# Feed-forward slabs whose weight sums are formed in place by accumulating transfers: 60 slabs a part in a staggered order, and the last tiles at half depth

## The chip, the cores and the metric

The kernel runs on one core of one Trainium2 chip. The metric is the device time of one execution in microseconds, lower is better. A core has TensorE (PE, matrix multiplication; PEld is its weight load), VectorE (DVE), ScalarE (ACT), GpSimd (POOL) and SyncE (SP). They run side by side, each taking its own instructions in a fixed order, and wait for each other through semaphores. Transfers are started by an engine's queue (here SP's, and POOL's where a transfer adds to what lies at its destination) and carried by sixteen DMA engines.

## What is computed

A trunk of two decoder layers on 256 tokens of width 2048. Layer 0 mixes tokens by causal pooling and attends to a memory; layer 1 uses differential attention over shared keys and values, and the memory again. Each layer ends in a squared-ReLU feed-forward part, which is what the change touches:

```
def squared_relu_mlp(h, w1, w2):
    z = jax.nn.relu(h @ w1)
    return (z * z) @ w2
...
x = x + squared_relu_mlp(rms_norm(x, ffn_norm[i]), w_ff1[i], w_ff2[i])
```

`w1` is 2048 x 8192 and `w2` 8192 x 2048, so `z` has 64 groups of 128 channels, and the result 16 groups.

## The kernel before

**Split numbers.** Each fp32 operand is used as a high part (rounded by a cast) and a low part (the rest). A product is high x high + high x low + low x high. Weights arrive in blocks of 128 x 128. Eight blocks make one 512 KB row of `wst`, the weights in order of use, which SP loads. ScalarE casts the high part into `hi_ring` (L178), VectorE subtracts to get the low part into `lo_ring` (L181). Each ring has six slots of 512 columns. A plain quad of four blocks takes one slot.

**Feed.** `Plan` records on a dry pass which quads and slab jobs are used in which order. `Feed.fill(job)` prepares a job and up to three entries ahead of it, as far as slots are free (`_prepare` L190, `fill` L225), and `Feed.load` (L122) issues the loads three or four rows ahead of that. The order of instructions on each engine is fixed when the program is built; the order in which the code writes them is its main input, and TensorE's instructions of neighbouring jobs can be interleaved.

**Plain tiles.** `up_tile` makes one group of 128 channels of `z` from 16 blocks of `w1` (`a_part`: for each block a 512-column matmul with the high weights, L433, and a 256-column one with the low weights, L435). What comes out of PSUM is copied (L761), summed, passed through ReLU and squared into one of the `stage` buffers, then split into `z` (`convert`). Two neighbouring groups of `z` also give four sums of quarters, split into `sit` (`combine`, L792-L803). `c_tile` (L447-L449) does a block in three 256-column matmuls that add up in one place, so nothing has to be summed after it.

**Slabs.** Most of `z @ w2` is computed by a two-by-two scheme with seven products in place of eight. A slab is a pair `i` of groups of `z` (256 channels) against 1024 columns of the result, the right half (group 0) or the left half (group 1). It holds four weight quarters of 128 x 512: left and right column quads for two channel groups. Its seven products, three matmuls of 512 columns each, add into seven PSUM banks, and are issued as four jobs: job 0 (two products, with the left column of quarters), job 1 (one product, with the sum T1), job 2 (two products, with the second sum T2 and one quarter), job 3 (two products). Before job 1 stands K, which makes T2 on VectorE (L204). The weight sums in the kernel before: T1 is made by a plain load and an accumulating transfer (`first_sum`, L153), T2 by K, the two operands of job 3 by one subtraction over 1024 columns after job 0's split (L218).

**Order.** The `up_tile` calls 0 to 63 make `z`; between their quarters `due` issues slab jobs by a table of due times in tiles (`early`, a constant rate, `late`). The jobs are slab after slab, 0 1 2 3. The same pairs serve both halves: four slabs of one group, then four of the other, and where the group changes, `swap` (L932, L924) copies the seven banks out to `keep` buffers and the other group's back. After the last slab of the left half `close_left` forms the left result, and `turn_left` transposes it into the residual. Pairs 0 to 23 are in both halves, 24 to 31 only in the right one: 56 slabs a part. The rest of the left half (eight tiles of 128 columns, channel groups 48 to 63) is done by `down_tile` at the end, in `last`, with the last sixteen slab jobs in between; `finish_banks` then forms the right half, and its transposes (L1016) and additions (L1017) follow eight and ten steps later. A step (`tick`) is one quad of blocks, or in `last` also one job.

Of the kernel before, what the change touches and what calls it, by code (L numbers as in the profile page):

```python
# [17 lines left out]
P = 128  # L18
T = 256
# [36 lines left out]
class Plan:  # L56
# [13 lines left out]
    def close(self):  # L70
        prep = []
        for job in self.jobs:

            if job[0] == "S" and job[2] == 0:
                prep.append(("K", job[1]))
            prep.append(job)
# [4 lines left out]
        for p in prep:  # L81
            if p[0] == "K":
                self.loads += [("S", p[1], 0), ("S", p[1], 1)]
            elif p[0] == "N" and p[1] % 2 == 0:
                self.loads.append(("N", p[1] // 2))
# [13 lines left out]
class Feed:  # L99


    def __init__(self, tc, wst, wpool, rows, plan, dry):
# [7 lines left out]
        self.t1 = None  # L110
        self.loads_ahead = LOADS
        self.t1_of = [None] * 3
# [9 lines left out]
    def load(self, upto):  # L122
        while self.lp < min(upto, len(self.plan.loads)):
# [6 lines left out]
            elif r[2] and r[1] % 2:  # L130
                t = self.spare
# [4 lines left out]
            elif r[2] == 0:  # L136
                if r[1] % PER_PART == 0:
                    self.first_sum(r[1])
                self.nc.sync.dma_start(t, self.wst[h])
                if (r[1] + 1) % PER_PART:  # L140
                    self.first_sum(r[1] + 1)
# [5 lines left out]
    def first_sum(self, n):  # L147
        i = n % len(self.t1)
        assert self.t1_of[i] is None
        self.t1_of[i] = n  # L150
        left, right = (self.wst[self.plan.row["S", n, c], :, 0:512] for c in range(2))
        self.nc.sync.dma_start(self.t1[i], left)
        self.nc.gpsimd.dma_start(self.t1[i], right, accum_op=ALU.add)  # L153
# [36 lines left out]
    def _prepare(self, p):  # L190
        sub, add = self.nc.vector.tensor_sub, self.nc.vector.tensor_add
# [9 lines left out]
        ra, rb = self.raw[("S", p[1], 0)], self.raw.get(("S", p[1], 1))  # L201
        t1 = self.t1[p[1] % len(self.t1)]
        if p[0] == "K":
            one = sub(rb[:, 0:512], t1, rb[:, 512:1024])  # L204
            if p[1] % PER_PART:
                self.order(one, self.last_low.ins.name)
# [5 lines left out]
        src, n = ((ra, 2), (t1, 1), (rb, 2), (ra, 2))[p[2]]  # L212
        if not self._split(p, src, n):
            return False
        if p[2] == 0:
            t2 = rb[:, 0:512].unsqueeze(1).to_broadcast([P, 2, 512])
            two = ra.rearrange("p (a c) -> p a c", a=2)
            sub(two, t2, two)  # L218
        if p[2] == 1:
            self.t1_of[p[1] % len(self.t1)] = None  # L220
        if p[2] == 3:
            del self.raw[("S", p[1], 0)], self.raw[("S", p[1], 1)]
# [69 lines left out]
def program(ctx, tc, plan, dry, xT, memT, par, lam, cst, wst, yT):  # L292
# [437 lines left out]
    def ffn(l, xs, tags, done):  # L730
# [12 lines left out]
        stage = [staged[:, T * j : T * j + T] for j in range(8)]  # L743
        sums = [room[:, 512 * j : 512 * j + 512] for j in range(2)]
        feed.t1 = [room[:, 1024 + 512 * j : 1536 + 512 * j] for j in range(3)]
        outs = [room[:, 2560 + 512 * j : 3072 + 512 * j] for j in range(2)]
        feed.spare = room[:, 3584:4608]
        keep = [room[:, 4608 + 512 * j : 5120 + 512 * j] for j in range(7)]
# [5 lines left out]
        z_done, sit_done = set(), set()  # L754
# [11 lines left out]
        def convert(j):  # L766
            a = stage[j % 8]
# [19 lines left out]
            def combine():  # L787
                sit_free[i % 4] = False
                a11, a21 = stage[2 * i % 8][:, 0:P], stage[2 * i % 8][:, P:T]
                a12, a22 = stage[(2 * i + 1) % 8][:, 0:P], stage[(2 * i + 1) % 8][:, P:T]  # L790
                s1, s2, s3, s4 = (sums[i % 2][:, c * P : c * P + P] for c in range(4))
                nc.vector.tensor_add(s1, a21, a22)  # L792
                nc.vector.tensor_sub(s3, a11, a21)
                nc.vector.tensor_sub(s2, s1, a11)
                nc.vector.tensor_sub(s4, a12, s2)
# [14 lines left out]
        def up_tile(i, ps, between=None):  # L810
# [18 lines left out]
            def square():  # L829
                nc.scalar.activation(stage[i % 8], y[:, 0:T], AF.Square)  # L830
# [4 lines left out]
        def down_tile(n, ps, between=None):  # L835
            ks = range(3 * NK, 4 * NK)
            if l == 1 and n == 7:
# [32 lines left out]
        def slab_jobs(g, i, again, end):  # L870
# [14 lines left out]
            def summed(c):  # L885
# [8 lines left out]
                ((5, lambda: summed(2)), (6, lambda: plain(1, 1))),  # L894
# [16 lines left out]
        def open_banks():  # L911
            tags = (("mm", 3), ("mm", 3), ("mm", 3), ("s", 2), ("s", 2), ("o", 1), ("t", 1))
            for p, (tag, bufs) in enumerate(tags):
# [739 lines left out]
```

## Time and profile before

| | us |
|---|---|
| median of three runs | 2005.55 (2004.99 to 2006.17) |
| the profiled execution | 2005.08 |
| its span, first to last instruction | 2003.3 |
| TensorE, VectorE, ScalarE, GpSimd busy | 1997.0, 1757.3, 1500.4, 149.9 |
| accumulating transfers | 112, each 256 KB |

A row of a timeline gives start, length, engine, line, operation, output<-input, shapes and count; in brackets the idle time before it and what ended it. A group row gives the count, then busy time and the mean of one in ns, then idle time before. A row of a stretch gives busy time and instruction count of each engine. Matmuls overlap, so the distance from one start to the next is their cost, not the length that a row prints. Lines such as L181 are lines of the kernel printed above.

### The profile page before, as it was taken

The page shows a single profiled execution, that of the slowest core. Times are in us where ns is not written, and L with a number is a line of the kernel's source. Part 1 is how long each engine was busy: PE and PEld are TensorE (multiplying, and loading weights), DVE is VectorE, ACT ScalarE, POOL GpSimd, SP SyncE. Part 2 cuts the span into 40 slices and gives each one's busy share as a digit, 9 for nine tenths or more (in the row PEclk, how much of TensorE's full clock was granted, in tenths as well). Part 3 has the DMA queues.
Part 4 walks back from the last instruction along what each step waited for, and adds up shares of the span by engine and source line. Part 5 has one row for each costly group of instructions (what it writes and reads, how often), then busy time and mean ns, then how long its engine had stood idle before and what let it go on. Part 6 is the DMA issues. An engine that isn't in the chain of part 4 may idle for free.

```text
span 2003.3 us, 31841 instructions
## 1 busy us (share of the span) xinstructions
PE 1997.0 (100%) x10534; PEld 1702.3 (85%) x10534; DVE 1757.3 (88%) x3089; ACT 1500.4 (75%) x2791; POOL 149.9 (7%) x179
## 2 busy tenths in 40 slices
PE   9999999999999999999999999999999999999999
PEld 8888888888888888888888888888888888888888
DVE  8888888989989899999765698878989899999987
ACT  7765577787887878778665699567787878888775
POOL 0001310000000000000000000320000000000000
PEclk9999999999999999999999999999999999999999
DMA  8555576777777776755566534567777777777764
GB/s 315 177 185 193 189 220 214 233 218 233 227 227 227 226 231 209 228 181 186 184 233 196 169 127 135 197 198 225 222 227 227 222 235 225 228 229 215 223 222 132
DMA packets 142725, 420.09 MB, mean 210 GB/s; under 512 B 16096, under 2 KB 18784, under 8 KB 142560
## 3 DMA queue, kind: packets, MB, share of 16 engines
q1 hardware_dynamic: 126288, 388.69, 57.9%
q0 software_dynamic: 16128, 29.37, 8.9%
q8 instruction: 82, 1.34, 0.3%
q14 instruction: 83, 0.68, 0.1%
q10 hardware_dynamic: 144, 0.01, 0.0%
HBM read 415.90 MB, written 2.10 MB: 209 GB/s over the span
## 4 chain that ended last, share of the span: by engine, by line
PE 97%; DVE 1%; ACT 1%; issue 0%; DMA 0%; DVEq 0%; ACTq 0%
PE x_bank L433 24%; PE x_bank L435 12%; PE p L865 9%; PE p L868 9%; PE p L867 9%; PE wo L433 6%; PE wo L435 3%; PE u L433 2%; PE ff L433 1%; PE u L435 1%; PE q L467 1%; PE q L469 1%; PE k L467 1%; PE q L468 1%; PE k L469 1%; PE v L467 1%
## 5 line engine op out<-in xcount | busy, mean ns | idle before, releaser
L178 ACT CAST hi_ring<-raw 128x512 fp32r<-128x512 f32 x1001 | 610.5, 621 | 270.4 <-PE x_bank L433 66.1
L181 DVE TENSOR_TENSOR lo_ring<-raw,hi_ring 128x512 fp32r<-128x512 f32 x1001 | 680.7, 695 | 109.0 <-ACT hi_ring L178 96.9
L433 PE MATMUL x_bank<-fx,hi_ring 128*128 128x512 f32 x1952 | 610.7, 394 | 0.0
L435 PEld LDWEIGHTS x_bank<-fx,lo_ring 128*128 128x128 f32 x1952 | 366.0, 188 | 86.2 <-DVE lo_ring L181 3.1
L181 DVE TENSOR_TENSOR lo_ring<-slab,hi_ring 128x1024 fp32r<-128x1024 f32 x280 | 342.2, 1222 | 58.0 <-ACT hi_ring L178 56.2
L178 ACT CAST hi_ring<-slab 128x1024 fp32r<-128x1024 f32 x280 | 294.3, 1052 | 121.6 <-PE x_bank L433 65.3
L435 PE MATMUL x_bank<-fx,lo_ring 128*128 128x256 f32 x1952 | 384.4, 278 | 0.2 <-DVE lo_ring L181 0.2
L433 PEld LDWEIGHTS x_bank<-fx,hi_ring 128*128 128x128 f32 x1952 | 318.1, 189 | 23.7 <-ACT room L761 1.6
L153 POOL DMA_DIRECT2D room<-in_w x112 | 96.8, 868 | 1127.5 <-DMA room<-in_w 1111.7
L865 PE MATMUL p<-hi_ring,sit 128*128 128x512 f32 x448 | 177.0, 395 | 0.7 <-ACT hi_ring L178 0.5
L867 PE MATMUL p<-hi_ring,sit 128*128 128x512 f32 x448 | 175.3, 391 | 0.0
L868 PE MATMUL p<-lo_ring,sit 128*128 128x512 f32 x448 | 174.5, 390 | 0.1
L433 PE MATMUL wo<-cat,hi_ring 128*128 128x512 f32 x512 | 161.8, 397 | 0.3 <-DVE rc L404 0.3
L181 DVE TENSOR_TENSOR lo_ring<-room,hi_ring 128x512 fp32r<-128x512 f32 x168 | 144.9, 864 | 6.9 <-ACT hi_ring L178 6.9
L178 ACT CAST hi_ring<-room 128x512 fp32r<-128x512 f32 x168 | 128.6, 766 | 23.7 <-PE x_bank L433 17.1
L865 PE MATMUL p<-hi_ring,z 128*128 128x512 f32 x336 | 131.3, 391 | 0.0
L867 PE MATMUL p<-hi_ring,z 128*128 128x512 f32 x336 | 131.1, 390 | 0.0
L868 PE MATMUL p<-lo_ring,z 128*128 128x512 f32 x336 | 130.7, 389 | 0.0
L435 PEld LDWEIGHTS wo<-cat,lo_ring 128*128 128x128 f32 x512 | 95.9, 188 | 22.0
L435 PE MATMUL wo<-cat,lo_ring 128*128 128x256 f32 x512 | 101.5, 279 | 0.0
L868 PEld LDWEIGHTS p<-lo_ring,sit 128*128 128x128 f32 x448 | 84.1, 188 | 20.3 <-DVE lo_ring L181 2.3
L865 PEld LDWEIGHTS p<-hi_ring,sit 128*128 128x128 f32 x448 | 84.0, 187 | 11.9 <-ACT hi_ring L178 3.3
(374 smaller groups left out, 3350.8 us busy)
## 6 DMA issues: line engine op xcount, KB each, us to landing
raw<-in_w SPq DMA_DIRECT2D x500, 512.0 KB, 4.3
slab<-in_w SPq DMA_DIRECT2D x112, 512.0 KB, 4.3
room<-in_w SPq DMA_DIRECT2D x168, 256.0 KB, 3.3
room<-in_w POOLq DMA_DIRECT2D x112, 256.0 KB, 5.8
slab<-in_w SPq DMA_DIRECT2D x56, 256.0 KB, 4.5
memraw<-in_mem SPq DMA_DIRECT2D x5, 512.0 KB, 4.5
resid<-in_x SPq DMA_DIRECT2D x8, 256.0 KB, 5.7
out_y<-resid SPq DMA_DIRECT2D x16, 128.0 KB, 1.9
```

What stands on the lines that cost most here:

```text
L153: self.nc.gpsimd.dma_start(self.t1[i], right, accum_op=ALU.add)
L178: self.last_cast = self.nc.scalar.copy(hi, src)
L181: low = self.nc.vector.tensor_sub(lo, src, hi.bitcast(F32))
L433: nc.tensor.matmul(ps, hi, xs[:, k, :], start=first and c == 0, stop=False)
L435: nc.tensor.matmul(ps[:, T : 2 * T], lo, xs[:, k, 0:T], start=False, stop=last and c == len(ks) - 1,)
L467: nc.tensor.matmul(ps[t], x[t][1], hi, start=k == 0, stop=False)
L468: nc.tensor.matmul(ps[t], x[t][0], hi, start=False, stop=False)
L469: nc.tensor.matmul(ps[t], x[t][0], lo, start=False, stop=k == NK - 1)
L865: nc.tensor.matmul(ps, a[1], hi, start=new, stop=False, **again)
L867: nc.tensor.matmul(ps, a[0], hi, start=False, stop=False, **again)
L868: nc.tensor.matmul(ps, a[0], lo, start=False, stop=end, **again)
```

## The change

Each slab keeps its sums in its own two buffers. Job 0's operand (left quarters, one above the other) is loaded plainly; after its split an accumulating transfer adds the right upper quarter to its first half, which then is T1. K adds T1 to the right lower quarter to form T2, in a buffer `second` (three of them) into which only the right lower quarter was loaded. After job 2's split a second accumulating transfer adds the right upper quarter to that half, and VectorE adds the left lower quarter to T2, so that job 3 finds its operands in place. Some signs of the sums of `z` and of the results change with it. The stage buffers are six instead of eight.

The jobs are staggered: a period holds job 0 of slab p+1, jobs 1 and 2 of slab p, and job 3 of slab p-1. Pairs 0 to 27 are in both halves, 28 to 31 only in the right: 60 slabs a part, with two more changes of the group. Periods are 0.97 tiles after the early ones. `down_tile` covers channel groups 56 to 63 only, tiles 3 to 7 in the three-matmul form; twelve jobs are left for `last`, in groups of 5, 3, 2 and 2 before tiles 0 to 3, and `finish_banks` stands before tile 3. Tile 4 of the up-projection uses another bank, and the slab banks are opened in two parts.

```diff
@@ class Plan, class Feed
-            if job[0] == "S" and job[2] == 0:
+            if job[0] == "S" and job[2] == 1:
                 prep.append(("K", job[1]))
...
-                if r[1] % PER_PART == 0:
-                    self.first_sum(r[1])
                 self.nc.sync.dma_start(t, self.wst[h])
-                if (r[1] + 1) % PER_PART:
-                    self.first_sum(r[1] + 1)
...
-    def first_sum(self, n):
-        i = n % len(self.t1)
-        assert self.t1_of[i] is None
-        self.t1_of[i] = n
-        left, right = (self.wst[self.plan.row["S", n, c], :, 0:512] for c in range(2))
-        self.nc.sync.dma_start(self.t1[i], left)
-        self.nc.gpsimd.dma_start(self.t1[i], right, accum_op=ALU.add)
+    def add_right(self, n, t):
+
+        h = self.plan.row["S", n, 1]
+        self.nc.gpsimd.dma_start(t, self.wst[h, :, 0:512], accum_op=ALU.add)
...
-            one = sub(rb[:, 0:512], t1, rb[:, 512:1024])
+            one = add(rb[:, 0:512], ra[:, 0:512], rb[:, 512:1024])
...
-        src, n = ((ra, 2), (t1, 1), (rb, 2), (ra, 2))[p[2]]
+        src, n = ((ra, 2), (ra, 1), (rb, 2), (rb, 2))[p[2]]
...
         if p[2] == 0:
-            t2 = rb[:, 0:512].unsqueeze(1).to_broadcast([P, 2, 512])
-            two = ra.rearrange("p (a c) -> p a c", a=2)
-            sub(two, t2, two)
+            self.add_right(p[1], ra[:, 0:512])
+        elif p[2] == 2:
+            self.add_right(p[1], rb[:, 512:1024])
+            add(rb[:, 0:512], rb[:, 0:512], ra[:, 512:1024])
...
@@ ffn
         def down_tile(n, ps, between=None):
-            ks = range(3 * NK, 4 * NK)
-            if l == 1 and n == 7:
+            ks = range(56, 64)
+            assert all(k in z_done for k in ks)
+            if n >= 3:
                 c_tile(ps, "w_ff2", l, n, ks, z)
...
-        for h in range(6):
-            for g in (0, 1) if h % 2 == 0 else (1, 0):
-                slabs += [(g, 4 * h + i, g == h % 2) for i in range(4)]
-        slabs += [(0, i, False) for i in range(24, 32)]
-        jobs = [(s, j) for s in range(len(slabs)) for j in range(4)]
+        for h, first in enumerate((0, 1, 0, 1, 0, 1, 1)):
+            for g in (first, 1 - first):
+                slabs += [(g, 4 * h + i, g == first) for i in range(4)]
+        slabs += [(0, i, False) for i in range(28, 32)]
+        early = (4.5, 6, 8, 10, 11.2, 12.2, 13.2, 14.2, 15.2, 16.2, 17.4, 18.4)
...
+            return 18.4 + 0.97 * (p - 10)
+
+        jobs = []
+        for p in range(-1, len(slabs) + 1):
+            for j, s in enumerate((p + 1, p, p, p - 1)):
+                if 0 <= s < len(slabs):
+                    when_due = tiles_at(p) + j * (tiles_at(p + 1) - tiles_at(p)) / 4
+                    jobs.append((when_due, s, j))
...
-        early = (4, 6, 8, 10, 11.5, 12.5, 13.5, 14.5, 15, 16, 17.5, 19, 20.5)
-        late = (58, 59.5, 61, 62.5, 64)
...
-        ends = (
-            (1, 1, 1, 0), (1, 1, 1, 0), (1, 1, 1, 1), (1, 0, 1, 0), (1, 0, 1, 0), (2, 0, 0, 0),
-        )
...
             for n in range(8):
-                if n < 6:
-                    some(ends[n][0])
-                if n == 5:
+                for c in range((5, 3, 2, 2, 0, 0, 0, 0)[n]):
+                    one_job()
+                    tick()
+                    if c == 2 and turns:
+                        turn_left(turns.pop(0))
+                assert n == 0 or not turns
+                if n == 3:
                     finish_banks()
-                ps = bank() if n < 6 else mmt("ff2")
-                down_tile(n, ps, between(n) if n < 6 else None)
+                down_tile(n, bank() if n < 4 else mmt("ff2"))
```

109 lines of the change are left out of this document (56 added, 53 removed).

## The prediction, made before the changed kernel was run

> **What bounds the kernel now.** First the profile page: its head, the row of engines, and the chain of work that ended last.
>
> ```profile
> span 2003.3 us, 31841 instructions
> ...
> PE 1997.0 (100%) x10534; PEld 1702.3 (85%) x10534; DVE 1757.3 (88%) x3089; ACT 1500.4 (75%) x2791; POOL 149.9 (7%) x179
> ...
> PE 97%; DVE 1%; ACT 1%; issue 0%; DMA 0%; DVEq 0%; ACTq 0%
> ```
>
> TensorE is idle for 6.3 us in all, and 97% of the chain is its own work. So the time moves by matmul time first, and then by gaps that the change opens. Second, the busy time of the engines by stretch (PE, PEld, DVE, ACT, POOL; then granted clock, DMA share, GB/s): the start of the first feed-forward part, the close of its left half, the end of that part, the middle of the second part.
>
> ```profile
> 260.00:300.00 40.00, 39.82 (x220) 34.14 (x219) 33.87 (x66) 29.37 (x58) 1.90 (x3) 1.00 0.73 206
> 750.00:800.00 50.00, 49.66 (x254) 41.09 (x253) 47.77 (x71) 43.24 (x73) 4.19 (x5) 1.00 0.70 215
> 910.00:920.00 10.00, 10.00 (x61) 8.76 (x60) 10.00 (x20) 7.68 (x15) 0.00 (x0) 1.00 0.63 201
> 1420.00:1820.00 400.00, 400.00 (x2056) 339.76 (x2055) 372.02 (x564) 321.76 (x542) 32.77 (x38) 1.00 0.76 228
> ```
>
> TensorE loses 0.18 us at the start and 0.34 us at the close, and nothing in 400 us of the middle, where VectorE is busy 93%, ScalarE 80% and the DMA engines 76%. At the end of the first part VectorE is at 100%. These are the engines that a change can run into.
>
> The profiled execution took 2005.08 us, 1.8 us more than its span; the median of the three runs is 0.47 us above it. I work out a difference and add it to the median, 2005.55.
>
> **Matmul time.** Rows of TensorE from the end of the second part: the first and, after twelve slab matmuls, the next row; the first of sixteen plain blocks and the row after them; the first block of a tile of three short matmuls per block, and its sixth following one.
>
> ```profile
> 1978.09 0.40 PE L865 MATMUL p<-hi_ring,sit 128*128 128x512 f32 x1
> ...
> 1980.82 0.61 PE L433 MATMUL x_bank<-z,hi_ring 128*128 128x512 f32 x2
> ...
> 1986.38 0.62 PE L433 MATMUL ff<-z,hi_ring 128*128 128x512 f32 x2
> ...
> 1991.96 0.27 PE L1016 MATMUL ct<-const,c_b 128*128 128x128 f32 x1
> ...
> 1993.19 0.28 PE L447 MATMUL ff<-z,hi_ring 128*128 128x256 f32 x1
> ...
> 1995.34 0.28 PE L447 MATMUL ff<-z,hi_ring 128*128 128x256 f32 x1
> ```
>
> Twelve slab matmuls take 2.73 us, so a slab's 21 take 4.78 us. Sixteen plain blocks take 5.58 us. A slab stands for 16 blocks: 0.80 us saved. There are four more slabs in each of two parts: **-6.4 us**. Five of the last eight tiles of each part now use the three-matmul form: 2.15/6 = 0.358 us a block against 0.349, on 80 blocks less the 8 that had it: **+0.7**.
>
> **VectorE and the steady stretch.** Each slab loses one subtraction over 1024 columns (L218) and gains one addition over 512; the K operation keeps its 512. Back to back they take (chain of waits, start and length):
>
> ```profile
> 762.26 0.60 DVE slab L204
> ...
> 763.46 1.14 DVE lo_ring L181
> ```
>
> That is 0.54 us less VectorE work a slab. Slabs now come every 0.97 tiles: 0.97 x 5.58 + 4.78 = 10.2 us, before every 1.04 tiles, 10.6. VectorE's 93% of 10.6 is 9.85; less 0.54 and some 0.3 for the shorter tile it is 9.0 of 10.2, 88%. TensorE had no gap here, so this gains nothing. SyncE issues two loads a slab instead of three; GpSimd issues two accumulating transfers instead of one. Those, from the view of their line and the page's queues:
>
> ```profile
> L153 POOL DMA_DIRECT2D room<-in_w x112: 853/862/1203, 256.9 to 1939.3; - x112
> L153 POOLq EVENT_SEMAPHORE  x106: 17/17/43, 256.2 to 1938.7; - x106
> ...
> DMA to landing us min/median/max: 3.6/5.8/8.5
> ```
>
> ```profile
> q1 hardware_dynamic: 126288, 388.69, 57.9%
> q0 software_dynamic: 16128, 29.37, 8.9%
> ```
>
> The queue releases the last one at 1938.7 and the issue starts at 1939.3: 0.6 us, then 5.8 us to landing. By the shares, an accumulated MB takes 8.9% x 2003 / 29.37 = 6.1 us of all engines, a plain one 3.0. In a 10.2 us period 0.52 MB and 1.80 MB make 8.6 us: 84% instead of 76%. From one low split through the accumulation to the next: 0.1 + 0.6 + 5.8 + a cast of 1.05 + a split of 1.22 = **8.8 us**. The staggered order leaves five jobs, 1.25 periods = 12.7 us, between job 0 and job 1 and between job 2 and job 3. So the second transfer is hidden here, by 3.9 us and the lead of the preparation; beyond that VectorE stands in its queue with the splits of the plain blocks behind it.
>
> Two more exchanges of the seven banks per part cost ScalarE fourteen copies each:
>
> ```profile
> L924 ACT COPY p<-room 128x512 f32<-128x512 f32 x56 | 33.0, 610 | 0.0
> L932 ACT COPY room<-p 128x512 f32<-128x512 f32 x56 | 31.7, 595 | 0.3
> ```
>
> 8.4 us each, where two periods leave some 4 us idle. In the 400 us above such exchanges cost nothing, at the close 0.34 us: four new ones cost 0 to 1.4, I take **+0.4**, nearer the many. At the start VectorE waited for the first sums:
>
> ```profile
> DVE slab L204 <- DMA room<-in_w: 10.6, 2, 5.4
> ```
>
> Now K of slab 0 comes two tiles after job 0, so the 0.2 us of TensorE go: **-0.2**. The same wait in the timeline:
>
> ```profile
> 259.39 0.40 ACT L386 ACTIVATE rs_t<-rs_h 128x256 f32<-128x256 f32 x1
> ...
> 263.92 0.69 DVE L204 TENSOR_TENSOR slab<-room,slab 128x512 f32<-128x512 f32 x1 [5.14 <-DMA room<-in_w]
> ...
> 264.53 0.42 DVE L329 SCALAR_TENSOR_TENSOR rs_t<-st_x,rs_t 128x256 f32<-128x256 f32 x1
> ```
>
> The operation at 264.53 was ready at 259.8 and stood behind it: the order on an engine is fixed beforehand, and did not foresee the landing.
>
> **The closing stretch** (59.2 is job 2 of slab 59, T0 to T7 the last tiles). The order is 58.0 57.1 57.2 56.3 59.0, T0, 58.1 58.2 57.3, T1, 59.1 59.2, T2, 58.3 59.3, sums, T3 to T7. Between the low matmuls of 59.2 and 59.3 lie only six matmuls (1.37), T2 (2.79) and six more (1.37): 5.5 us against a chain of 8.8. What covers the rest is how early 59.2's split is done. Three low splits of a job 2, each with the first matmul that reads it (first, one of the middle, last of 112):
>
> ```profile
> 279.25 1.22 DVE L181 TENSOR_TENSOR lo_ring<-slab,hi_ring 128x1024 fp32r<-128x1024 f32 x1
> 283.27 0.39 PE L868 MATMUL p<-lo_ring,sit 128*128 128x512 f32 x1
> ...
> 712.73 1.21 DVE L181 TENSOR_TENSOR lo_ring<-room,hi_ring 128x1024 fp32r<-128x1024 f32 x1
> 715.23 0.39 PE L868 MATMUL p<-lo_ring,sit 128*128 128x512 f32 x1
> ...
> 1975.68 1.22 DVE L181 TENSOR_TENSOR lo_ring<-room,hi_ring 128x1024 fp32r<-128x1024 f32 x1 [0.51 <-ACT hi_ring L178]
> 1978.55 0.39 PE L868 MATMUL p<-lo_ring,sit 128*128 128x512 f32 x1
> ```
>
> The leads are 2.8, 1.3 and 1.65 us, mean 1.9. 8.8 - 5.5 - 1.9 = 1.4 us a part: **+2.8**. Behind 59.3 in TensorE's queue stand T3's matmuls, on the other two engines T3's splits. Bounds: a landing at 3.6 gives 0, no lead 3.3 a part, a landing at 8.5 with the mean lead 4.1.
>
> VectorE from 58.0 to the split of 59.3: eight splits of 1.14, eight of 0.60, eight more 512-column operations, eight of 256 columns and four of 128:
>
> ```profile
> 266.08 0.34 DVE z L776
> ```
>
> ```profile
> L792 DVE TENSOR_TENSOR room<-stage 128x128 f32<-128x128 f32 x64 | 18.3, 286 | 5.4 <-ACT stage L830 5.4
> ```
>
> 9.1 + 4.8 + 4.8 + 2.7 + 1.1 = 22.5 us. TensorE has 13.0 (jobs) + 0.5 + 8.4 (T0 to T2) + 0.9 (two transposes of the left half) = 22.8. That is 99%; before, sixteen jobs lay among six full tiles. Between 0 (the lead covers it) and the lost lead, 1.9 a part, I take 0.4: **+0.8**.
>
> The last eight transposes now come after T7, since T3 to T7 make only ten steps:
>
> ```profile
> 1992.12 0.87 PE ct L1016 x8
> ```
>
> ```profile
> 1999.32 0.28 PE L449 MATMUL ff<-z,lo_ring 128*128 128x256 f32 x1
> ...
> 1999.64 0.42 DVE L840 TENSOR_TENSOR room<-ff,r_x 128x256 f32<-128x256 f32 x1 [2.01 <-PE ff L449]
> 2000.10 0.42 DVE L841 TENSOR_TENSOR resid<-resid,room 128x256 f32<-128x256 f32 x1
> ```
>
> Now 1.2 us lead from the last matmul to the last addition. After: 0.6 for four transposes and their wait, two additions of 0.60, then T7's two, 0.9: 2.7. Less the 0.87 of transposes that left the path: **+0.7**, in the second part alone.
>
> **Sum:** -6.4 + 0.7 - 0.2 + 0.4 + 2.8 + 0.8 + 0.7 = -1.2, so **2004.3 us**.
>
> The Trainium skill, page "DMA: Bandwidth & Descriptors", section "Anatomy of one DMA — SWDGE (gpsimd) path", gives such a transfer about 2.0 us plus its bytes at 436 GB/s, 2.6 us for 256 KB as an estimate. The row above says 5.8 at the median and never under 3.6, so the trace does not agree. By that figure the wait before 59.3 would vanish and the sum be 2.8 us lower.
>
> **Rivals.**
>
> *In time.* A landing of 4.4 us or less at 59.3, or T3's matmuls placed before it, removes the 2.8, and with it VectorE's 0.8. For it: the minimum of 3.6, and a DMA share of only 43 to 63% at the end of a part. Against it: the median of 5.8, and the order that did not foresee the landing at the start. 2004.3 - 3.6 = 2000.7 us.
>
> *VectorE has no lead at the close* (slower). It decides when VectorE's work in the closing stretch exceeds TensorE's: at 99%, a few waits for ScalarE do it. Then each 59.3 costs 1.9 more (+3.8), and in the first part, where twelve tiles' splits for the next layer at 0.40 add 4.8 us and VectorE is at 100% already, half of these are not hidden (+2.4). 2010.5 us. Against it: TensorE lost nothing at 910 to 920, at that same 100%.
>
> *The transfers queue* (slower). At 84% the landing would have to grow from 5.8 to over 11 us for the steady stretch to wait; the longest of 112 is 8.5. If a third of the 120 slabs waited 0.4 us, +16: 2020 us.
>
> **Numbers.** My forecast 0.43, in time 0.30, no lead 0.21, queueing 0.06. This kernel's measurement can tell about 0.2%, 4.0 us, from no change. My forecast's own range is 2001 to 2008, nearly all of it no change; faster is the first rival and 0.03 of the forecast, 0.33; slower the two others, 0.27. The range 1999.6 to 2010.8 leaves out the queue, the upper half of the no-lead case and the lowest part of the first rival.
>
> **What would show it.** Products: 60 slabs at 4.78 us. A ScalarE or VectorE wait for an accumulating transfer about 20 us before the end of a part, with a TensorE gap of 1 to 2 us, shows the term of 59.3; no such gap, and 2000 to 2001, shows the first rival; VectorE at 100% there with gaps at several jobs, the second; long landings and waits in mid-part, the third. If the middle's gaps are not near 0, the step that the stagger hides the transfers is wrong.

## The result, and the profile after

The changed kernel takes 2009.41 us (median of 13 runs, 2007.76 to 2012.57) against 2005.40 us for the kernel before (13 runs beside it, 2004.32 to 2006.50): a ratio of 1.0020, 95% interval 1.0013 to 1.0028. The forecast was 2004.3. The profiled execution took 2008.45 us, with a span 3.2 us longer than before's. One of the executions behind this document, at a granted clock of 0.654, took 2822.13 us; it belongs to experiment 6, whose ratio leaves it out.

First the page of the changed kernel: its head, the row of engines, the two queues, and the chain.

```profile
span 2006.5 us, 32110 instructions
...
PE 1991.4 (99%) x10510; PEld 1697.4 (85%) x10510; DVE 1728.1 (86%) x3096; ACT 1526.8 (76%) x2838; POOL 260.9 (13%) x307
...
q1 hardware_dynamic: 110160, 357.22, 54.2%
q0 software_dynamic: 34560, 62.93, 19.0%
...
PE 68%; issue 22%; POOL 4%; ACT 2%; DMA 2%; DVE 1%; POOLq 0%; SPq 0%; DVEq 0%; ACTq 0%
```

TensorE's busy time fell by 5.6 us and the span still grew: TensorE is now idle for 15.1 us and not 6.3. TensorE's own work was 97% of the chain and is 68%, but that is no measure of the loss: another 22% of the chain is "issue", in which an engine on it waited for nothing that the profile shows, while TensorE is idle for less than 1% of the span. VectorE has less to do in all (1728.1 against 1757.3 us). So the question is where the idle time lies, and it lies in few places. From the starts of the first matmuls of each stage in both traces:

| stage, us | before | after | difference |
|---|---|---|---|
| start, to the first feed-forward matmul | 251.56 | 251.19 | -0.4 |
| first feed-forward part, to the first `k` matmul | 675.62 | 675.05 | -0.6 |
| `k` tiles, to the first `v` matmul | 67.60 | 70.45 | +2.85 |
| the rest, to the second part | 328.75 | 328.77 | 0.0 |
| second part, to the last matmul | 675.78 | 675.72 | -0.1 |
| from there to the end of the span | 4.0 | 5.3 | +1.35 |

The first part has 20 matmuls of 512 columns fewer and 16 of 256 columns more. The second, where one tile had three matmuls a block before, has 4 and 16 fewer. At 0.227 and 0.116 us from start to start that is -2.7 and -2.8 us, -5.4 in all, where the prediction had -5.7. So some 2 to 2.6 us a part are given back inside the parts, and 4.2 us behind them. The busy time by stretch (PE, PEld, DVE, ACT, POOL; granted clock, DMA share, GB/s) of the changed kernel shows the places:

```profile
440.00:460.00 20.00, 18.73 (x95) 15.32 (x94) 17.39 (x29) 13.81 (x24) 3.46 (x4) 1.00 0.84 227
...
910.00:920.00 10.00, 8.68 (x71) 8.26 (x71) 10.00 (x21) 7.80 (x16) 0.00 (x0) 1.00 0.37 116
924.00:934.00 10.00, 8.68 (x49) 7.27 (x48) 9.87 (x23) 7.96 (x18) 0.00 (x0) 1.00 0.29 106
...
1515.00:1535.00 20.00, 18.88 (x95) 15.43 (x94) 17.17 (x29) 13.84 (x24) 3.46 (x4) 1.00 0.87 233
1975.00:1985.00 10.00, 8.36 (x42) 6.37 (x41) 7.69 (x13) 6.18 (x11) 0.86 (x1) 1.00 0.54 144
```

Five stretches, and two kinds. At 910 and 924, around the end of the first part, VectorE is full (10.00 and 9.87 of 10). At 440, 1515 and 1975 TensorE waits though VectorE is not full: something is late there. The two in mid-part were not expected at all.

The stall at 450, in TensorE's timeline, then ScalarE's (start, length, engine, line, operation, and in brackets the idle time before it and who ended it):

```profile
450.10 0.39 PE L867 MATMUL p<-lo_ring,sit 128*128 128x512 f32 x1
450.97 0.50 PE L864 MATMUL p<-hi_ring,z 128*128 128x512 f32 x1 [0.48 <-ACT hi_ring L176]
451.30 0.40 PE L866 MATMUL p<-hi_ring,z 128*128 128x512 f32 x1
452.48 0.50 PE L867 MATMUL p<-lo_ring,z 128*128 128x512 f32 x1 [0.79 <-DVE lo_ring L179]
```

```profile
445.47 1.05 ACT L176 CAST hi_ring<-room 128x1024 fp32r<-128x1024 f32 x1 [1.45 <-PE p L866]
449.35 0.62 ACT L176 CAST hi_ring<-raw 128x512 fp32r<-128x512 f32 x1 [2.83 <-DMA raw<-in_w]
449.87 1.04 ACT L176 CAST hi_ring<-room 128x1024 fp32r<-128x1024 f32 x1
```

The matmuls wait for the cast from `room` at 449.87 (a job 3), and that cast was ready; it stood on ScalarE behind the cast of a plain row, which waited 2.83 us for its transfer. Start to start, TensorE lost 1.60 us here and 1.45 us at 1524.

The wait before 59.3 in the second part, which the prediction had, on ScalarE:

```profile
1978.30 0.62 ACT L176 CAST hi_ring<-raw 128x512 fp32r<-128x512 f32 x1 [1.08 <-issue]
1981.47 1.04 ACT L176 CAST hi_ring<-room 128x1024 fp32r<-128x1024 f32 x1 [2.54 <-DMA room<-in_w]
```

TensorE was idle for 1.35 us before 1982.56 and 0.29 before 1983.82; from start to start it lost 2.0 us. In the first part there is no such gap. Over the whole kernel three casts waited for one of the 240 accumulating transfers, all three in a closing stretch (896.60, 905.69 and this one); from the view of the transfers' line:

```profile
  ACT hi_ring L176: 3.7, 3
...
DMA to landing us min/median/max: 3.6/5.5/8.1
```

The end of the first part. TensorE, then VectorE just ahead of the second gap:

```profile
917.06 0.33 PE L1015 MATMUL ct<-const,c_b 128*128 128x128 f32 x1 [0.68 <-DVE c_a L1004]
918.03 0.33 PE L1015 MATMUL ct<-const,c_a 128*128 128x128 f32 x1 [0.64 <-ACT c_a L967]
...
932.81 0.73 PE L466 MATMUL k<-lo_ring,x_kv 128*128 128x512 f32 x2 [1.32 <-DVE lo_ring L179]
```

```profile
928.74 1.28 DVE L1016 TENSOR_TENSOR resid<-resid,ct 128x512 f32<-128x512 f32 x2
930.14 1.68 DVE L326 SCALAR_TENSOR_TENSOR x_kv<-resid,param,x_kv 128x256 fp32r<-128x256 f32 x4
931.75 0.42 DVE L839 TENSOR_TENSOR room<-ff,r_x 128x256 f32<-128x256 f32 x1
932.08 0.68 DVE L179 TENSOR_TENSOR lo_ring<-raw,hi_ring 128x512 fp32r<-128x512 f32 x1
```

First the transposes wait for the final sums and their scaling (1.70 us from start to start, in two gaps). Then, once they are done, their additions and the low halves of `x_kv` come in one lump, 3.4 us of VectorE, and the low split that the next `k` matmul needs is the last of the four lines.

### The profile page after: what moved, and what is told of

The parts are those of the page before. It is cut to its first block, busy times and chain, and to the rows that moved or that the text cites. A ratio compares the mean times of both kernels' runs of the same rounds, so it can differ in the third digit from the quotient of the medians.

```text
span 2006.5 us, 32110 instructions
## 1 busy us (share of the span) xinstructions
PE 1991.4 (99%) x10510; PEld 1697.4 (85%) x10510; DVE 1728.1 (86%) x3096; ACT 1526.8 (76%) x2838; POOL 260.9 (13%) x307
## 4 chain that ended last, share of the span: by engine, by line
PE 68%; issue 22%; POOL 4%; ACT 2%; DMA 2%; DVE 1%; POOLq 0%; SPq 0%; DVEq 0%; ACTq 0%
PE x_bank L430 13%; PE x_bank L432 7%; PE wo L430 6%; PE p L864 5%; PE p L867 5%; PE p L866 5%; PE wo L432 3%; PE u L430 2%; POOL room L151 2%; POOL slab L151 2%; PE ff L430 1%; PE u L432 1%; PE q L464 1%; PE q L466 1%; PE q L465 1%
## 5 line engine op out<-in xcount | busy, mean ns | idle before, releaser
L176 ACT CAST hi_ring<-raw 128x512 fp32r<-128x512 f32 x969 | 595.2, 620 | 258.7 <-PE wo L430 58.7
L179 DVE TENSOR_TENSOR lo_ring<-raw,hi_ring 128x512 fp32r<-128x512 f32 x969 | 663.9, 694 | 111.2 <-ACT hi_ring L176 99.3
L179 DVE TENSOR_TENSOR lo_ring<-room,hi_ring 128x1024 fp32r<-128x1024 f32 x240 | 293.2, 1222 | 50.8 <-ACT hi_ring L176 47.2
L176 ACT CAST hi_ring<-room 128x1024 fp32r<-128x1024 f32 x240 | 252.8, 1053 | 91.1 <-PE p L866 50.0
L179 DVE TENSOR_TENSOR lo_ring<-slab,hi_ring 128x512 fp32r<-128x512 f32 (+1 forms) x240 | 228.9, 954 | 50.8 <-ACT hi_ring L176 48.3
L176 ACT CAST hi_ring<-slab 128x512 fp32r<-128x512 f32 (+1 forms) x240 | 199.9, 834 | 52.0 <-PE p L866 27.2
L864 PE MATMUL p<-hi_ring,sit 128*128 128x512 f32 x480 | 188.8, 393 | 0.0
L866 PE MATMUL p<-hi_ring,sit 128*128 128x512 f32 x480 | 187.6, 391 | 0.0
L867 PE MATMUL p<-lo_ring,sit 128*128 128x512 f32 x480 | 187.0, 390 | 0.0
L151 POOL DMA_DIRECT2D slab<-in_w x120 | 104.0, 867 | 603.6 <-DVE lo_ring L179 591.0
L864 PE MATMUL p<-hi_ring,z 128*128 128x512 f32 x360 | 141.6, 393 | 2.2 <-ACT hi_ring L176 2.2
L866 PE MATMUL p<-hi_ring,z 128*128 128x512 f32 x360 | 140.7, 391 | 0.0
```

What stands on the lines that cost most here:

```text
L151: self.nc.gpsimd.dma_start(t, self.wst[h, :, 0:512], accum_op=ALU.add)
L176: self.last_cast = self.nc.scalar.copy(hi, src)
L179: low = self.nc.vector.tensor_sub(lo, src, hi.bitcast(F32))
L864: nc.tensor.matmul(ps, a[1], hi, start=new, stop=False, **again)
L866: nc.tensor.matmul(ps, a[0], hi, start=False, stop=False, **again)
L867: nc.tensor.matmul(ps, a[0], lo, start=False, stop=end, **again)
```

## The experiments

Each ran beside the kernel before on the same chip, ten executions (nine of one); ratios are to the kernel before, whose medians in these sessions lie between 2005.28 and 2005.58 us.

**1. The order of loads on SyncE.** The first theory for the mid-part stalls came from the view of waits on SP's queue:

```profile
SPq L142 <- DVE room L215: 300.8, 98, 8.0
```

A slab row load waits up to 8.0 us for the new addition (L215) to read out its buffer, and raw rows stand behind it.

```
 # Plan.close, for slabs 3 to 57 of a part
...
+self.loads.insert(i, self.loads.pop(e))   # e: the next raw row, i: the slab row before it
...
```

> SyncE's queue issues each slab's next row load one place later, behind the raw row that follows it. Theory (the queue's order): the stalls of 1.6 us at 450 and 1.45 us at 1524 come from a raw row that stands behind a slab row load, which waits up to 8.0 us for its buffer to be read out by the new VectorE addition; both stalls go, the matmul starts around them run without a break, and the time falls by 2.5 to 3.1 us to about 2006.6. Rival (the DMA engines): they are busy 0.84 to 0.87 of the 20 us around the stalls, a raw row needs 6.4 us there whatever stands in front of it, and the stalls stay or move by a tile: 2008.9 to 2009.9.

2008.12 us, 1.0016 [1.0007, 1.0025]. Both stalls stayed, at the same matmul and within 0.1 us of their size (the first of them):

```profile
450.55 0.50 PE L877 MATMUL p<-hi_ring,z 128*128 128x512 f32 x1 [0.37 <-ACT hi_ring L189]
450.88 0.40 PE L879 MATMUL p<-hi_ring,z 128*128 128x512 f32 x1
452.06 0.51 PE L880 MATMUL p<-lo_ring,z 128*128 128x512 f32 x1 [0.78 <-DVE lo_ring L192]
```

The theory falls. The median is 1.3 us below the changed kernel's all the same: a difference of that size between two of these medians says little without the traces. The rival, that the DMA engines are too busy, predicted that they stay, but so does anything that is fixed when the program is built. What decides is a detail: the row on which the cast waits was issued at 442.90 and landed at 449.33, yet the cast of that row's first half comes only at 463.46. This one is its second half. ScalarE's instructions at the place, in the order in which the built program has them (numbers of rows in the order of loading):

```
raw row 161, first half     -> ring slot 4
slab, job 2                 -> slots 0, 1
raw row 167, second half    -> slot 5        <- the cast at 449.35
slab, job 3                 -> slots 2, 3
raw row 161, second half    -> slot 4
slab row 162, job 0         -> slots 0, 1
raw row 163, first half     -> slot 2
```

Row 167's cast stands ahead of thirteen casts that the code writes before it (the expectation below counts eleven, within twelve places). A job of two slots does not fit into slot 5 alone and wraps to slot 0; slot 5 stays empty, so the later cast that gets it has nothing to wait for but its row, and the order that is fixed at build time moves it forward. In the changed kernel 85 casts stand ahead of an earlier one, this one and its like at 1523.46 farthest; in the kernel before there are 52, none of them over four places ahead.

**2. The accumulating transfer before 59.3.** For slab 59 alone, the right upper quarter is loaded early by SyncE into a spare block and added by VectorE.

```
...
-            self.add_right(p[1], rb[:, 512:1024])
+            if p[1] % 60 == 59:
+                add(rb[:, 512:1024], rb[:, 512:1024], self.extra)
+            else:
+                self.add_right(p[1], rb[:, 512:1024])
...
```

> For the last slab of each part alone (59) the second accumulating transfer is replaced by a plain early load into a spare buffer and one more VectorE addition of 128x512. Theory (the transfer's latency): in the second part the cast waited 2.54 us for that transfer and the matmuls 1.35 + 0.29 us; this goes, in the first part nothing changes, the time falls by 1.3 to 1.9 us to about 2007.8. Rival (the engines' work in the closing stretch): VectorE is busy 9.7 to 10 of 10 us around, the addition costs it another 0.6 us, and the same wait comes back as one for VectorE: 2009.0 to 2010.0.

2007.09 us, 1.0011 [1.0001, 1.0020]: 2.3 us less than the changed kernel. From the first slab matmul of the second part to its last, 630.9 us against 633.0, -2.1. In the first part this stretch is 0.35 us shorter, but the transposes behind it lost 0.5 (their waits grew from 1.70 to 2.19). The transfer's latency it was, and VectorE's extra addition did not bring the wait back.

**3. The squares after the first part.**

```
-        at(2 + n // 2, lambda n=n: later_square(n))
+        at(5 + n // 2, lambda n=n: later_square(n))
-    at(12, lambda: c1.extend(columns("x")))
+    at(15, lambda: c1.extend(columns("x")))
```

> The squares of the residual and the columns of the norm are put three k steps later, into the first kv tile. Theory (a VectorE backlog after the first part): the first kv matmuls wait 1.49 us at 931 and 0.83 us at 947 for VectorE's low halves, which stand behind the split gains, tile additions and squares; with the squares later the 1.49 us falls to under 0.7 and the 0.83 us goes or moves: 1.0 to 2.0 us less, about 2007.9. Rival (what stands in front of the low halves is the closing's own work, not the squares): 931 stays at 1.3 to 1.5 us and the columns are now late for the key rows: 2008.8 to 2010.5.

2009.68 us, 1.0021 [1.0012, 1.0031]. The gap at 931 stayed at 1.48 us, the one at 947 became 1.38 with 0.32 behind it. The rival holds: what stands ahead of the split are the additions and splits of the late transposes, as the four VectorE lines above show, and not the squares.

**4. 56 slabs with the rest of the change.** Sums in place, two accumulating transfers and staggered jobs stay; the slabs and the depth of the last tiles are those of before, and the pace is 1.02 tiles a slab, then 1.3.

```
-        for h, first in enumerate((0, 1, 0, 1, 0, 1, 1)):
+        for h, first in enumerate((0, 1, 0, 1, 0, 1)):
-            return 18.4 + 0.97 * (p - 10)
+            return 18.4 + 1.02 * (min(p, 48) - 10) + 1.3 * max(p - 48, 0)
-            ks = range(56, 64)
+            ks = range(3 * NK, 4 * NK)
-            if n >= 3:
+            if l == 1 and n == 7:
...
```

> Sums in place, second accumulation and staggered jobs stay, but each part has 56 slabs again and its last eight tiles their whole depth of 16 (jobs paced at 1.02 tiles, then 1.3). Theory (the shorter closing gives the gain back): the matmul time of before comes back (+6.4 us), the gaps of the closing (0.64 + 1.7 in the first part, 1.9 + 0.5 in the second), of the layer's boundary (2.85) and of the tail (1.35) go, and the stalls of the steady stretch (3.0) stay unless the pace changes them: 2004.5 to 2008. Rival (steady stretch and stagger are not at fault and neither is the closing; only the matmul time counts): 2009.4 + 6.4 = 2015.8. Rival (the second transfer costs in the steady stretch throughout): more than 2010, with gaps spread over the whole part.

2005.62 us, 0.9996 [0.9987, 1.0005], but spread from 2001.44 to 2007.29. The matmul time of before is back, and still it is 3.8 us faster than the changed kernel. In its profile all gaps of the close and of the boundary are gone: no gap over 0.1 us in the 29.8 us from the last slab matmul to the first `k` matmul, which were 17.8 in the changed kernel, and 67.61 us of `k` tiles, as in the kernel before. The two stalls in mid-part are absent as well, which the expectation had left in.

**5. Casts in order.** `order` adds a dependency that only fixes the sequence on an engine; it is used from the first slab on.

```
-        self.last_cast = self.nc.scalar.copy(hi, src)
+        one = self.nc.scalar.copy(hi, src)
+        if self.slab_no:
+            self.order(one, self.last_cast.ins.name)
+        self.last_cast = one
```

> Each cast of the ring is put behind the cast before it on ScalarE; nothing else changes. New theory (a cast out of its order): at 449.35 and 1523.46 ScalarE's queue holds a cast of a raw row ahead of eleven casts that are needed earlier, in a ring slot that was left empty where the ring wraps; that row was only issued at 442.90 and 1517.16 and landed 6.3 to 6.4 us later, and the casts that the matmuls need stand behind it. In order, both stalls (1.60 and 1.45 us) go: 2.5 to 3.1 us less than the changed kernel, about 2006.5. Rival (the DMA engines or the ring's depth are the limit there): the stall comes back at another cast within the next tile, 2008.9 to 2009.9. Rival (casts out of order were of use elsewhere, 85 of them): many small gaps of 0.1 to 0.3 us appear, over 2010.

2007.13 us, 1.0009 [1.0000, 1.0019]: 2.3 us less than the changed kernel. Both stretches are whole; the two windows, and ScalarE at the place:

```profile
440.00:460.00 20.00, 20.00 (x104) 17.04 (x103) 18.54 (x31) 14.89 (x24) 3.45 (x4) 1.00 0.91 240
1515.00:1535.00 20.00, 20.00 (x105) 17.06 (x104) 18.67 (x29) 14.63 (x25) 3.45 (x4) 1.00 0.94 245
```

```profile
445.12 1.05 ACT L176 CAST hi_ring<-room 128x1024 fp32r<-128x1024 f32 x1 [1.30 <-PE p L869]
447.19 1.06 ACT L176 CAST hi_ring<-room 128x1024 fp32r<-128x1024 f32 x1 [1.02 <-PE p L869]
448.57 0.62 ACT L176 CAST hi_ring<-raw 128x512 fp32r<-128x512 f32 x1 [0.33 <-PE x_bank L433]
```

The cast from `room` comes 2.7 us earlier (2.3 counted from the start of the part) and TensorE is never late, with the DMA engines at 0.91 and 0.94 of their time: they had not been the limit at 0.84. Not all of the 3.05 us is gained: summed over the two parts, TensorE's gaps over 0.03 us fall only from 12.8 to 12.3 us between the two traces, so some 2.5 us come back, most of it as new gaps of 0.2 to 0.4 us elsewhere. The second rival has a part in it, though its time of over 2010 did not come. The two profiled executions differ by 1.5 us, the medians by 2.3.

The same edit with the plain load of slab 59:

> The casts in order and the plain early load for the last slab together. If the two causes are separate, the gains add: 3.0 + 2.3 below the changed kernel, 2003.5 to 2004.8, which is 0.3 to 0.9 us or more below the kernel before. If the closing stretch is held by VectorE whatever is done to the stalls, 2006 to 2007.

2005.75 us, 1.0002 [0.9993, 1.0012]: 3.7 us below the changed kernel, of the 4.6 that the two give alone, and between the two times that were expected. No gap over 0.4 us is left in mid-part or at 59.3, and the kernel is level with the one before, although its matmul time is 5.4 us shorter. The largest waits that its profile still shows are 2.2 us at the transposes of the first part and 2.4 us in the `k` stage. That profile is of the slowest of its ten executions, 2007.89 us, so its waits are at the upper end.

**6. Final sums one tile earlier.** On the last kernel:

```
-                for c in range((5, 3, 2, 2, 0, 0, 0, 0)[n]):
+                for c in range((5, 3, 4, 0, 0, 0, 0, 0)[n]):
-                if n == 3:
+                if n == 2:
```

> As the one with the casts in order and the plain load, and the last twelve jobs stand before the first three of the last eight tiles as 5, 3, 4 and not before four as 5, 3, 2, 2, so that the final sums begin one tile (2.86 us of matmul) earlier. Theory (the close is too short for the chain from the last job to the last addition): the transposes no longer wait (1.7 us in the first part, 0.47 in the second), the tail after the last matmul goes back from 5.3 to about 4.0 us, VectorE's backlog into the kv tiles shrinks: 2.5 to 4.5 us below the one without, about 2000.5. Rival (four jobs packed before one tile wait for their casts, as VectorE is busy 9.7 to 10 of 10 us): new gaps of 1 to 2 us before the third tile take most of it, 2003 to 2005.

2006.10 us, 1.0002 [0.9993, 1.0012]: nothing gained, and slower than the theory and its rival had it. The transposes no longer wait and the time from the start of the last matmul to the end of the span is 3.9 us and not 5.2. But 0.85 us are lost before 903.5 and 1.13 before 1979, at the packed jobs, and the boundary got worse. Its stretches there:

```profile
918.00:922.00 4.00, 4.00 (x37) 4.00 (x36) 4.00 (x9) 2.68 (x7) 0.00 (x0) 1.00 0.67 201
922.00:926.00 4.00, 4.00 (x33) 3.79 (x31) 3.94 (x9) 3.65 (x9) 0.00 (x0) 1.00 0.17 67
926.00:928.50 2.50, 0.36 (x2) 0.00 (x0) 2.50 (x7) 1.69 (x5) 0.00 (x0) 1.00 0.66 210
928.50:930.00 1.50, 1.31 (x4) 1.09 (x5) 1.50 (x4) 0.49 (x1) 0.00 (x0) 0.78 0.00 0
930.00:932.00 2.00, 2.00 (x6) 1.58 (x5) 1.94 (x6) 1.37 (x4) 0.00 (x0) 0.50 0.38 84
```

VectorE pauses for 0.06 us from 918 to 930, while TensorE stands idle from 926.4 to 928.7. The wait moved, the load did not. In two of these rows the granted clock is below 1; the last section comes back to that.

**7. VectorE relieved.** In the two kernels above, the low halves of the last eight chunks of the first part's output are made by GpSimd, from one more ScalarE copy.

```
...
+        nc.scalar.activation(w, src, AF.Copy, scale=g)
+        nc.gpsimd.tensor_sub(dst[:, T : 2 * T], w, dst[:, 0:T].bitcast(F32))
...
```

> As casts in order with the plain load for slab 59, and the low halves of the last eight chunks of the first part's output are made by GpSimd from one more ScalarE copy: 8 VectorE instructions of 0.48 us (3.9 us) less in the stretch from 908 to 935. Theory (VectorE's queue is the bound at the layer's boundary): the wait of 1.56 us at 933 falls below 0.6 and the one at 949 (0.80) with it or by half, 1.0 to 2.3 us less, about 2004; the transposes' waits at 916 (1.08 + 1.11) stay, as only two of these instructions stand ahead of them. Rival (what is late is the chain of sums, scaling and transposes, not VectorE's load): the wait at 933 stays above 1.3, 2005.5 to 2006.5; GpSimd's subtraction, 0.7 to 1.0 us each by its nearest rows, may be late for the kv steps and add to it.

> The same relief in the kernel whose final sums begin one tile earlier. There VectorE was busy in all of 918 to 922 and 926 to 930, the matmuls waited 2.5 us at 926 and the granted clock was 0.78, 0.50 and 0.81 in the next three stretches. Theory (VectorE's queue): the 2.5 us falls below 1.0, the clock stays at 1.0, 2.5 to 4 us less, 2002 to 2003.6. Rival (the wait is for something else that follows the transposes): 2005.5 to 2006.5.

2005.35 us, 1.0001 [0.9991, 1.0010], and 2004.55 us, 0.9995 [0.9986, 1.0005]. In the first of them the wait of 1.56 us at the boundary became 0.54 with 0.32 behind it, and the later one went from 0.80 to 0.29, while the transposes kept their 1.09 + 1.10: together 1.2 us, of which the median shows 0.4. The fall of the first wait is clear: in the six kernels of 60 slabs with the same close and no relief it is 1.48 to 1.57 us. The later one proves little, since in five of these six it lies anywhere from under 0.15 to 0.83 us (1.38 with the squares moved). In the second kernel the 2.5 us became 0.68 with another 0.67 behind it, which is a wait for a cast of ScalarE, the granted clock stayed at 1.00, and the median fell by 1.55 us, less than expected. So VectorE's queue is what the `k` matmuls wait for at the boundary. GpSimd takes its place only in part; that it slows VectorE meanwhile (last section) may be one reason.

**8. The two better halves together.** The kernel of experiment 4 with its casts in order.

> The kernel of 56 slabs with sums in place and stagger, and its casts in order. Its times lay in two groups, 2001.4 to 2002.5 and 2005.6 to 2007.3, and its profile, from the lower group, shows gaps of 0.63 at 592 and 0.31 at 684 at casts that stand ahead of their order and wait for an accumulating transfer. Theory (casts out of order wait for transfers that land late in some executions): with the order kept the upper group goes, median 2000.5 to 2002.5. Rival (the upper group is the transfers' own delay, whatever the order): both groups stay, median 2003 to 2006.

2000.42 us, 0.9975 [0.9965, 0.9985], nine executions between 2000.29 and 2000.60: faster than both kernels, and the upper group of times is gone. Without the order ScalarE's casts waited 22 times for an accumulating transfer, 25.4 us in all, in an execution of the lower group; with it, never. Its page and three stretches:

```profile
span 1998.6 us, 31872 instructions
```

```profile
440.00:460.00 20.00, 20.00 (x105) 17.06 (x104) 19.00 (x32) 14.95 (x26) 3.45 (x4) 1.00 0.90 236
880.00:930.00 50.00, 50.00 (x281) 43.40 (x280) 48.73 (x96) 38.02 (x76) 0.86 (x1) 1.00 0.62 192
930.00:994.00 64.00, 64.00 (x294) 53.19 (x293) 48.85 (x110) 45.14 (x90) 0.00 (x0) 1.00 0.58 185
```

TensorE has no gap at the close or at the boundary, with VectorE at 97% of the 50 us ahead of it.

**9. The order alone.** Is it only the order that helps?

> The kernel before with its casts in order and nothing of the change. It has 52 casts out of order, none more than four places. If the gain of the 56-slab kernel over the kernel before (5.2 us) comes from the order alone: 2000 to 2002. If it comes from the stagger and the sums in place, which the order only sets free: 2004.3 to 2005.6, the small gaps at 766 to 778 and 1838 to 1850 (1.68 us together) at most gone.

2005.99 us, 1.0001 [0.9991, 1.0010]: no. The order alone does nothing for the kernel before, the change at 56 slabs without the order gives 0.9996, and both together give 0.9975. Which part of that change does it (sums in place, stagger, pace, the last jobs ahead of whole tiles) no run separates. Summed from the traces, TensorE's gaps over 0.15 us are 1.5 and 1.3 us in the two parts before and 0.8 in each part of the 56 slabs in order, those from 0.03 to 0.15 us 2.4 and 2.8 against 1.0 and 1.2. That is the 2.1 and 2.0 us by which its parts are shorter at the same matmul count. Why the small gaps of the kernel before are there was not tried.

## Why the prediction was wrong, point by point

The forecast was 1.2 us less than the kernel before, and the change took 4.0 us more.

- **Matmul time (-6.4 + 0.7).** Right: -5.4 us by the counted matmuls.
- **Start wait (-0.2) and bank exchanges (+0.4).** Small, as said: the gaps at the first slab (0.34 and 0.22 us) are gone, and no exchange in the steady stretch leaves a gap over 0.15 us. Some 0.6 us are lost in each part at 897 and 1971, where TensorE waits for a copy of ScalarE (L757). The kernels of 56 slabs do not have these gaps; why the copy is late was not tried.
- **"The second transfer is hidden here", TensorE without a gap in mid-part.** Here the prediction failed for the first time. The transfers were hidden: they landed in 3.6 to 8.1 us, median 5.5, and ScalarE waited for three of the 240, 3.7 us in all, none of them in mid-part. But TensorE lost 1.60 and 1.45 us to a plain row, because a cast stood out of its order. The prediction put gaps in mid-part at nothing. It had quoted a case of an order that "did not foresee the landing" and drew no price from it for ScalarE's casts, though jobs of two slots in a ring of six came in a new sequence. Its own sign, gaps in the middle, would have put the blame on the transfers, which were not the cause. Experiments 1 and 5 separate this from the queue on SyncE and from the DMA engines. The two shares worked out for the steady stretch came out right: from 1420 to 1820 VectorE is busy 89% and the DMA engines 85%, where 88 and 84% stood.
- **Wait before 59.3 (+2.8).** The mechanism was right, the place in part: 2.0 us in the second part, next to nothing in the first, 2.3 us by experiment 2.
- **VectorE in the closing stretch (+0.8).** This is the second step that failed. It was called 99% full from 58.0 to 59.3 and priced at 0.4 us a part; what comes after 59.3 was left out of the sum. The work that overflowed was behind it: the final sums ran late and the transposes waited (1.70 us and 0.47), their additions and splits came as a lump onto the first `k` tiles (+2.85 us over the `k` stage): 5.0 us where 0.8 stood. The rival "VectorE has no lead at the close" described this in kind, and was set at 0.21 for a reason that did not hold: at the same 100% of VectorE TensorE had lost nothing before. That its 2010.5 us came so near the 2009.4 measured is in part luck: it put 3.8 us more on the two 59.3, which did not come, and it did not have the 3.05 us of mid-part. The busy share did not tell the two cases apart: from 910 to 920 VectorE is at 100% in the kernel before, which loses nothing there, and in the changed kernel, which loses 1.3 us. How far its queue was ahead of TensorE there, the prediction did not read. With the longer close of experiment 4 every one of these gaps is gone.
- **Tail (+0.7).** Right in kind; it measured 1.35 us.
- **The transfers queue.** It did not come: the longest landing is 8.1 us against 8.5 before, at 84 to 87% of the DMA engines.

What the prediction did not have at all is a gain. The new gaps named here add up to over 8 us in the two parts, yet the gaps there grew by only 4.8 us (over 0.03 us, from 8.0 to 12.8), so over 3 us of small gaps of the kernel before are gone.

So the change is two things of opposite sign. With casts in order, 60 slabs take 6.7 us longer than 56 (2007.13 against 2000.42) although their matmuls are 5.4 us shorter. By the two traces these 12 us are 4.6 us more of gaps (over 0.03 us) in the first part, 3.8 in the second, 2.2 in the `k` stage and 1.3 in the tail. What stays open: why the kernel of 56 slabs without the order had times up to 2007.29, since its one profile is of the lower group; that the order takes them away is shown, through which cast is not.

## What to carry to other kernels

A saving in matmul time that shortens the end of a stage must be priced against the chain from the last product to the next stage's first operand, and an engine that was full but ahead before is the first to look at. When a ring of buffers with pieces of two sizes wraps, look in the built order of the engine that fills it for work moved ahead into the slot that was left empty: here one such cast behind a late load held up TensorE for 1.6 us, and a dependency that keeps the order took the stall away. Test the parts of a change apart: here the part that looked auxiliary was worth 5 us once the casts were kept in order, and the part with the saving cost more than it saved.

## What the runs showed of the hardware

**The clock falls after a short wait.** In experiment 6 TensorE was idle for 2.3 us at the boundary. The granted clock was 0.78 in the next 1.5 us and 0.50 in the 2 us after that, and matmuls of 512 columns started 0.43 us apart, not 0.23. The twelve from 928.69 on took 4.45 us instead of 2.7, so the wait cost 1.7 us more than its length:

```profile
928.69 0.50 PE L474 MATMUL k<-hi_ring,x_kv 128*128 128x512 f32 x1 [2.33 <-DVE room L850]
...
930.03 0.63 PE L474 MATMUL k<-hi_ring,x_kv 128*128 128x512 f32 x1
930.46 0.63 PE L475 MATMUL k<-hi_ring,x_kv 128*128 128x512 f32 x1
```

The Trainium skill, page "TensorE: Matmul & The Clock Gate", section "Part 1: The HAM clock gate (the "warmup" mystery)", has the half clock after an idle window of about 3.4 us; here 2.3 us without a matmul were enough. Less can be enough, and need not be: in the kernel with casts in order and the plain load, two waits of 1.1 us at the transposes were followed by a clock of 0.63 from 920 to 924, and the same two waits in its sibling with GpSimd's help by 1.00.

```profile
920.00:924.00 4.00, 4.00 (x25) 4.00 (x25) 3.40 (x8) 1.97 (x4) 0.00 (x0) 0.63 0.75 255
```

```profile
920.00:924.00 4.00, 4.00 (x36) 4.00 (x36) 3.70 (x9) 2.69 (x5) 0.00 (x0) 1.00 0.83 255
```

The first fence is of the one, the second of the other: 25 matmuls in the same 4 us against 36.

The thirteen executions of the changed kernel fit this. The five with a mean granted clock of 1.000 took 2007.76 to 2008.61 us, the four with 0.999 took 2008.65 to 2010.77, and the four with 0.998 took 2009.49 to 2012.57. By the middle one of the five, 2008.33 us, some 1 us of the median's 4.0 above the kernel before goes with the lower clock, as an estimate; which came first there, longer waits or the clock, no trace tells.

**GpSimd slows VectorE.** In the second kernel of experiment 7 GpSimd made its eight subtractions in one run, and some of VectorE's rows beside it are about twice as long as those just before:

```profile
923.05 7.55 POOL L1347 TENSOR_TENSOR x_kv<-wide,x_kv 128x256 fp32r<-128x256 f32 x8 [28.66 <-ACT wide L1346]
```

```profile
922.36 0.44 DVE L851 TENSOR_TENSOR resid<-resid,room 128x256 f32<-128x256 f32 x1
922.70 0.71 DVE L186 TENSOR_TENSOR lo_ring<-raw,hi_ring 128x512 fp32r<-128x512 f32 x1
923.30 1.30 DVE L1027 TENSOR_TENSOR resid<-resid,ct 128x512 f32<-128x512 f32 x2
...
926.76 0.95 DVE L851 TENSOR_TENSOR resid<-resid,room 128x256 f32<-128x256 f32 x1
927.64 1.23 DVE L186 TENSOR_TENSOR lo_ring<-raw,hi_ring 128x512 fp32r<-128x512 f32 x1
928.79 0.41 DVE L850 TENSOR_TENSOR room<-ff,r_x 128x256 f32<-128x256 f32 x1
```

0.44 became 0.95 and 0.71 became 1.23 us, in rows that read two tiles in SBUF. The rows that read one input from PSUM (`ct` and `ff`) kept their length: 1.30 us for two in this run and 1.30 just before it (920.24), 0.41 and 0.44. The Trainium skill, page "GPSIMD Engine Reference", section "1. Specifications", says that the two engines share their way to SBUF and get into each other's way when VectorE has two inputs there; the trace agrees. That may be part of why the relief was worth less than the 3.9 us of instructions that it took away; no run separates it.
